# Token and unit transposes and slot products moved inside the gate/up and down groups of neighbouring experts

## The chip, the cores and the metric

The kernel runs on one NeuronCore of one Trainium2 chip. The metric is the device time of one launch in microseconds (us), lower is better; a profiled execution of the same program gives the trace.

## What is computed

One layer of a decoder trunk on 512 tokens of width 1024: a token mixer (an mLSTM branch and a latent attention branch, gated), cross-attention into 256 memory tokens, and a mixture of experts, each followed by a residual and a LayerNorm. All of it is in f32. The change lies in the mixture of experts, which is, in short:

```python
logits = xt @ w_router + b_router
top_val, top_idx = lax.top_k(logits, 4)
gate = softmax(top_val)
def expert(x, e):
    gu = x @ w_gu[e] + b_gu[e]
    glu, lin = gu[..., ::2], gu[..., 1::2]
    glu = minimum(glu, 7.0)
    lin = clip(lin, -7.0, 7.0)
    u = glu * sigmoid(1.702 * glu) * (lin + 1.0)
    return u @ w_dn[e] + b_dn[e]
```

Each of the 512 tokens goes to 4 of 32 experts; the experts' rows are weighted by the gate and added to the token. How many tokens an expert gets is known only at run time; on average it is 64.

## The kernel before

The first third of the span computes the mixer, the cross-attention and the router; the change leaves it alone. Then `experts` goes through the experts e = 0 to 31 in one unrolled loop, with down products one expert late (f = e - 1). The loop stands in a manual schedule: on PE, VectorE (DVE), ScalarE (ACT) and GpSimd (POOL) instructions run in the order in which the code issues them. Weights come in slabs of 128 x 1024 f32 (512 KB), 16 of gate/up and 8 of down for each expert, through a ring of 36 buffers (named raw, whi, wlo) that SP fills in the order of use; a buffer is free again when its last product has run.

The steps of one pass of the loop, with the lines of the code before:

- `up` (L1090): gate/up products of expert e, tokens stationary, weights streaming, in four quarters of two k each. An expert's tokens are cut into parts of 64, 32, 32 and 64; all but the first are inside branches on the token count (over 64: L1105, over 96: L1107, over 128: L1109). The result lies in four PSUM buffers of the tag gu, and for the last part in two of the tag y (tiles gux).
- `tokens` (L1059): PE transposes the gathered rows xg of expert e + 1 (tile xt), ACT copies them to xe. Second and third part are in branches (L1068, L1070).
- `routing` and `route_expert`: sixteen small products with one-hot matrices give the places and gates of expert e + 2 (tile sl; "slots" below), DVE reads them; POOL makes the next one-hots. `conds` then loads the next token count into registers of each engine (L1228).
- `gather` by POOL into xg for expert e + 2.
- `units` (L1121): DVE and ACT turn gate/up results into units (tiles mg, ml, mlx), the parts beyond 64 tokens first, each in its branch (L1126, L1127, L1128).
- `down` (L1168): down products of expert f into y, y2 (tag y) and y3, yx (tag gu), in two halves of four k each, with the same cuts by token count (L1172, L1174, L1176).
- `hidden` (L1135): PE transposes the units of expert e (tile ht), ACT copies them to hs, the stationary operand of the next down.
- `rows_out` (L1179): ACT and DVE add up the rows of expert f (tile ysb), POOL scatters them into the output sum.

PSUM has two buffers each of the tags y and tp (transposes and slots take tp) and four of gu, so that down's y is the bank that gate/up's overflow part had just before. A branch that is not taken lets the engine's sequencer wait for the work before it and signal in its place; the trace names such a releaser with a q (DVEq L1126, PEq L1107).

Of the kernel before, what the change touches and what calls it, by code (L numbers as in the profile page):

```python
# [109 lines left out]
class Trunk:  # L110
# [976 lines left out]
                for h in range(2):  # L1087
                    self.bias(e, n, h, j, out(h, j))

    def up(self, rv, e, x, w):  # L1090

        tc = self.tc
        b = [self.ps("gu", "gu") for _ in range(4)]
        bm = [self.ps("gux", "y") for _ in range(2)]

        def two(b):
            return lambda h, j: b[j][64 * h:64 * h + 64]

        def four(b):
            return lambda h, j: b[64 * j + 32 * h:64 * j + 32 * h + 32]  # L1100

        for q in range(4):
            ks = (2 * q, 2 * q + 1)
            self.up_part(e, ks, 64, x[:, :, 0:64], w, two(b))
            with tc.If(rv > 64):  # L1105
                self.up_part(e, ks, 32, x[:, :, 64:96], w, four(b[2]))
                with tc.If(rv > 96):  # L1107
                    self.up_part(e, ks, 32, x[:, :, 96:128], w, four(b[3]))
                    with tc.If(rv > 128):  # L1109
                        self.up_part(e, ks, 64, x[:, :, 128:192], w, two(bm))  # L1110
        return b, bm

    def some_units(self, g, l, pg, pl, by=1.0):
# [4 lines left out]
        nc.vector.tensor_scalar(l, pl, 8.0, -6.0, op0=OP.min, op1=OP.max)  # L1118
        nc.vector.scalar_tensor_tensor(l, l, by, g, op0=OP.mult, op1=OP.mult)

    def units(self, rv, b, bm, twice):  # L1121

        tc = self.tc
        g = self.mx.tile([128, 512], F32, name="mg", tag="mg", bufs=1)
        l, l2, lx = [self.mx.tile([128, 512], F32, name=n, tag=n, bufs=1) for n in ("ml", "ml2", "mlx")]
        with tc.If(rv > 64):  # L1126
            with tc.If(rv > 96):  # L1127
                with tc.If(rv > 128):  # L1128
                    self.some_units(g, lx, *bm)
                self.some_units(g[64:128], l2[64:128], b[3][0:64], b[3][64:128])  # L1130
            self.some_units(g[0:64], l2[0:64], b[2][0:64], b[2][64:128])
        self.some_units(g, l, b[0], b[1], twice)
        return l, l2, lx

    def hidden(self, rv, l, l2, lx):  # L1135
# [26 lines left out]
                r = 64 * (k % 2) + 32 * n  # L1162
                self.nc.tensor.matmul(o[r:r + 32], h[:, k], w(k)[:, ts(n, 512)], start=k < 2, stop=k > 5)  # L1163

    def down(self, rv, h, w):
        tc = self.tc
        y, y2 = [self.ps("y", "y") for _ in range(2)]
        y3, yx = [self.ps("yx", "gu") for _ in range(2)]  # L1168
        for q in range(2):
            ks = range(4 * q, 4 * q + 4)  # L1170
            self.down_64(ks, y, h[:, :, 0:64], w)
            with tc.If(rv > 64):  # L1172
                self.down_32(ks, y2, h[:, :, 64:96], w)
                with tc.If(rv > 96):  # L1174
                    self.down_32(ks, y3, h[:, :, 96:128], w)
                    with tc.If(rv > 128):  # L1176
                        self.down_64(ks, yx, h[:, :, 128:192], w)
        return y, y2, y3, yx

    def rows_out(self, rv, few, p, route):  # L1180
# [46 lines left out]
    def cond(self, c, *engines):  # L1227
        return self.nc.values_load(c[0:1, 0:1], engines=engines, min_val=0, max_val=512,  # L1228
                                   skip_runtime_bounds_check_because="a count of the 512 tokens")

    def experts(self):
        nc, tc, a = self.nc, self.tc, self.a
        p, cond = self.mx, self.cond
        PE, DVE, ACT, POOL = (mybir.EngineType.PE, mybir.EngineType.DVE, mybir.EngineType.Activation, mybir.EngineType.Pool)
        self.more_x = p.tile([64, 1024], F32, name="mrxg", bufs=1)
        nc.gpsimd.memset(self.more_x, 0.0)
        self.ys = [p.tile([128, 1024], F32, name=f"ysb{i}", bufs=1) for i in range(2)]
        for y in self.ys:
            nc.gpsimd.memset(y, 0.0)

        order = []
        for e in range(33):
            order += [(e, h, k) for k in range(8) for h in range(2) if e < 32]
            order += [(e - 1, 2, k) for k in range(8) if e]
        slabs, self.nfetch = {}, 0

        def fetch(n):

            for e, part, k in order[self.nfetch:self.nfetch + n]:
                slabs[e, part, k] = self.slab(a["wdn"][e, k] if part == 2 else a["wgu"][e, part, k])  # L1250
            self.nfetch += n

        def number(e):

            c = self.mx.tile([1, 1], I32, name="number", tag="number", bufs=4)
            nc.gpsimd.tensor_copy(c, self.count[0:1, e:e + 1])
            return c

        def conds(c):
            return cond(c, PE, ACT), cond(c, DVE, ACT), cond(c, POOL), cond(c, PE)  # L1260

        def more_gather(e):
            with tc.If(rv[e][2] > 128):
                self.gather(self.more_x, route[e][1][0])

        def routing(e):
            route[e] = self.route_expert(e, self.mx, self.oh)
            if e < 31:
                count[e + 1] = number(e + 1)
                self.oh = self.one_hots(e + 1, self.mx)  # L1270

        count = {0: number(0), 1: number(1)}
        route, rv, h = {0: self.first}, {0: conds(count[0])}, {}
        self.bias_rows()
        fetch(len(self.ring["s"][0]))
        more_gather(0)
        x = self.tokens(rv[0][0])
        self.oh = self.one_hots(1, self.mx)
        with tc.manual_schedule(engines={PE, DVE, ACT, POOL}):
            routing(1)  # L1280
            rv[1] = conds(count[1])
            self.gather(self.xg, route[1][0][0])
            more_gather(1)
            for e in range(33):
                f = e - 1
                if e < 32:
                    b, bm = self.up(rv[e][3], e, x, lambda h, k: slabs[e, h, k])
                    fetch(16)
                if e < 31:
                    x = self.tokens(rv[e + 1][0])  # L1290
                if e < 30:
                    routing(e + 2)
                    rv[e + 2] = conds(count[e + 2])
                    self.gather(self.xg, route[e + 2][0][0])
                    more_gather(e + 2)
                if e < 32:
                    l = self.units(rv[e][1], b, bm, route[e][2])
                if 0 < e:
                    out = self.down(rv[f][3], h[f], lambda k: slabs[f, 2, k])
                    fetch(8)  # L1300
                if e < 32:
                    h[e] = self.hidden(rv[e][0], *l)
                if 0 < e:
                    self.rows_out(rv[f][1], rv[f][2], out, route[f])
        self.overflow()

    def overflow(self):
# [174 lines left out]
```

## Time and profile before

| | us |
|---|---|
| median of 3 runs (lowest to highest) | 1924.85 (1924.28 to 1926.68) |
| profiled execution, its own time | 1923.97 |
| span of its trace | 1922.3 |
| PE busy | 1717.8 |
| DVE busy | 623.8 |
| ACT busy | 462.7 |
| POOL busy | 299.5 |

The mean granted TensorE clock over the span is 0.953 of full speed; HBM is read and written at 271 GB/s on average. The expert loop takes the stretch from about 629 to 1886. PE's idle time is listed in the trace with what ended it; PE busy is no measure of PE at its peak, since matmuls overlap and their time depends on the granted clock.

### The profile page before, as it was taken

To read this page: it belongs to the slowest core of one execution; us is meant where nothing else is said; L and a number is where in the kernel's file an instruction comes from. 1 tells how busy PE (TensorE), PEld (TensorE's weight loads), DVE (VectorE), ACT (ScalarE), POOL (GpSimd) and SP (SyncE) were. 2 spreads that over 40 slices of the span, in tenths; PEclk is the share of its full clock that TensorE was granted. 3 is DMA by queue.
4 is the path that set the end of the run, shared out by engine and by line. 5 is a ranking of instruction groups with operands and counts; after the bars stand their busy time and mean duration, and the time that the engine had idled before them with its cause. 6 is when DMAs were issued, how large, how long until landed. Compare 5 with 4: busy or idle time off the path is not lost. (4 is left out here: it accounts for less than half of the span.)

```text
span 1922.3 us, 26305 instructions
## 1 busy us (share of the span) xinstructions
PE 1717.8 (89%) x9564; PEld 854.1 (44%) x9564; DVE 623.8 (32%) x1319; ACT 462.7 (24%) x882; POOL 299.5 (16%) x413
## 2 busy tenths in 40 slices
PE   8998999999996788989999888888988898998892
PEld 6666888778975222332332232223322333233230
DVE  7855776467564212111121111111111102122113
ACT  5567555345431201110111111001001101111001
POOL 1000003420012212111101121112111112011202
PEclk9999999999997899999999999999999999999996
DMA  4213334655234999998657999899998998678973
GB/s 165 93 61 115 97 108 159 197 189 187 83 119 156 383 404 389 383 378 327 231 191 273 364 361 354 322 364 368 396 355 330 387 353 309 207 264 303 397 268 116
DMA packets 149257, 504.88 MB, mean 263 GB/s; under 512 B 21648, under 2 KB 24240, under 8 KB 149040
## 3 DMA queue, kind: packets, MB, share of 16 engines
q1 hardware_dynamic: 131632, 459.86, 63.9%
q0 software_dynamic: 17408, 42.02, 7.7%
q8 instruction: 150, 2.46, 0.5%
q14 instruction: 67, 0.55, 0.1%
HBM read 486.84 MB, written 33.29 MB: 271 GB/s over the span
## 5 line engine op out<-in xcount | busy, mean ns | idle before, releaser
L1084 PE MATMUL gu<-raw,xe 128*64 128x512 f32 (+1 forms) x2624 | 516.0, 600 | 24.2 <-PEq L1107 10.6
L1084 PEld LDWEIGHTS gu<-raw,xe 128*64 128x64 f32 (+1 forms) x2624 | 153.4, 127 | 337.3 <-issue 308.6
L1156 PE MATMUL y<-raw,hs 128*64 128x512 f32 x920 | 254.5, 701 | 31.4 <-DVEq L1127 8.2
L998 DVE TENSOR_REDUCE gs<-sl 128x1 f32<-128x3 f32 x32 | 5.1, 161 | 665.5 <-PE sl L996 665.4
L984 POOL TENSOR_SCALAR oh<-places,pm 128x192 bf16<-128x192 bf16 x128 | 97.2, 789 | 548.7 <-PE sl L996 527.4
L1065 ACT COPY xe<-xt 128x512 f32<-128x512 f32 x50 | 27.8, 588 | 596.6 <-PE xt L1056 596.6
L1156 PEld LDWEIGHTS y<-raw,hs 128*64 128x64 f32 x920 | 76.5, 160 | 191.9 <-issue 142.6
L1017 POOL DMA_INDIRECT based<-ysb,ixm x32 | 51.5, 1611 | 477.4 <-ACT ysb L1205 417.4
L128 DVE TENSOR_TENSOR wlo<-raw,whi 128x1024 fp32r<-128x1024 f32 (+2 forms) x81 | 86.9, 1075 | 45.2 <-ACT whi L128 44.9
L1141 ACT COPY hs<-ht 128x512 f32<-128x512 f32 (+1 forms) x55 | 26.5, 510 | 309.3 <-PE ht L1056 309.3
L128 ACT CAST whi<-raw 128x1024 fp32r<-128x1024 f32 (+2 forms) x81 | 75.4, 932 | 80.6 <-issue 19.0
L1084 PE MATMUL gu<-wlo,xe 128*64 128x512 f32 (+1 forms) x368 | 87.8, 594 | 3.3 <-PEq L1107 2.3
L1084 PE MATMUL gu<-whi,xe 128*64 128x512 f32 (+1 forms) x336 | 80.6, 602 | 5.6 <-PEq L1147 1.8
L1117 ACT ACTIVATE mg<-mg 128x512 f32<-128x512 f32 (+1 forms) x55 | 34.6, 630 | 127.2 <-DVE mg L1116 119.7
L1192 DVE TENSOR_TENSOR ysb<-ysb,y 32x512 f32<-32x512 f32 x30 | 20.4, 680 | 137.8 <-ACT ysb L1191 137.6
L1163 PE MATMUL y<-raw,hs 128*32 128x512 f32 x440 | 57.6, 598 | 0.0
L160 PE MATMUL g<-xTh,wlo 128*128 128x512 f32 x128 | 52.4, 410 | 2.8 <-DVE wlo L128 2.8
L158 PE MATMUL g<-xTh,whi 128*128 128x512 f32 x128 | 52.5, 410 | 0.0
L159 PE MATMUL g<-xTl,whi 128*128 128x512 f32 x128 | 52.0, 406 | 0.0
L1116 DVE TENSOR_SCALAR mg<-gu 128x512 f32<-128x512 f32 (+1 forms) x52 | 35.8, 689 | 47.0 <-ACTq L1126 18.3
L1084 PEld LDWEIGHTS gu<-wlo,xe 128*64 128x64 f32 (+1 forms) x368 | 25.2, 125 | 57.0 <-issue 53.2
L1204 DVE COPY ysb<-y 64x512 f32<-64x512 f32 x32 | 21.8, 683 | 80.5 <-PE y L1156 75.6
(494 smaller groups left out, 2793.3 us busy)
## 6 DMA issues: line engine op xcount, KB each, us to landing
raw<-in_wgu SPq DMA_DIRECT2D x406, 512.0 KB, 8.4
raw<-in_wdn SPq DMA_DIRECT2D x230, 512.0 KB, 10.1
wlo<-in_wgu SPq DMA_DIRECT2D x53, 512.0 KB, 10.0
whi<-in_wgu SPq DMA_DIRECT2D x53, 512.0 KB, 10.1
raw<-in_wt SPq DMA_DIRECT2D x27, 512.0 KB, 3.8
whi<-in_wdn SPq DMA_DIRECT2D x13, 512.0 KB, 10.5
wlo<-in_wdn SPq DMA_DIRECT2D x13, 512.0 KB, 10.0
tgd<-tg POOLq DMA_DIRECT2D x16, 256.0 KB, 2.8
```

The costliest lines, as they stand in the source:

```text
L128: return nc.scalar.copy(hi, src).ins, (lo_eng or nc.vector).tensor_sub(lo, src, hi.bitcast(F32)).ins
L158: mm(out, w[0], x[0], start=start, stop=False)
L159: mm(out, w[0], x[1], start=False, stop=False)
L160: mm(out, w[1], x[0], start=False, stop=stop)
L984: self.nc.gpsimd.tensor_scalar(oh[:, b], self.places, self.pm[:, b, e:e + 1], None, op0=OP.is_equal)
L1017: self.nc.gpsimd.indirect_dma_start(out=self.based, out_offset=bass.IndirectOffsetOnAxis(ap=ix[:, 0:1], axis=0), in_=y, in_offset=None, bo ...
L1065: nc.scalar.copy(x[:, :, c:c + n], self.turned(src, 8, "xt", first).rearrange("p (k t) -> p k t", t=n))
L1084: mm(out(h, j), x[:, k], w(h, k)[:, ts(j, 512)], start=k == 0, stop=False)
L1116: nc.vector.tensor_scalar(g, pg, 7.0, None, op0=OP.min)
L1117: nc.scalar.activation(g, g, AF.Gelu_apprx_sigmoid)
L1156: self.nc.tensor.matmul(o[64 * n:64 * n + 64], h[:, k], w(k)[:, ts(n, 512)], start=k == 0, stop=k == 7)
L1163: self.nc.tensor.matmul(o[r:r + 32], h[:, k], w(k)[:, ts(n, 512)], start=k < 2, stop=k > 5)
```

## The change

`up` takes a table of work to do behind its quarters, `units` and `down` take one function to call in their middle. Pass e of the loop then runs: first quarter of gate/up of e; unit transposes of f (`turn_units`); second and third quarter; slots of e + 2 (`next_slots`); fourth quarter; first half of down of f; units of e on DVE and ACT, and among them the token transposes of e + 1 and the gather of e + 2 (`next_tokens`); second half of down of f; rows of f. `units` now converts the part beyond 128 tokens first, in a branch of its own, then the first 64, and the parts between after the function has been called. The last unit transposes stand alone in the pass e = 32.

```diff
-    def up(self, rv, e, x, w):
+    def up(self, rv, e, x, w, between):
...
+            for work in between.get(q, ()):
+                work()
         return b, bm
...
-    def units(self, rv, b, bm, twice):
+    def units(self, rv, b, bm, twice, between):
...
+        with tc.If(rv > 128):
+            self.some_units(g, lx, *bm)
+        self.some_units(g, l, b[0], b[1], twice)
+        between()
         with tc.If(rv > 64):
+            self.some_units(g[0:64], l2[0:64], b[2][0:64], b[2][64:128])
             with tc.If(rv > 96):
-                with tc.If(rv > 128):
-                    self.some_units(g, lx, *bm)
                 self.some_units(g[64:128], l2[64:128], b[3][0:64], b[3][64:128])
-            self.some_units(g[0:64], l2[0:64], b[2][0:64], b[2][64:128])
-        self.some_units(g, l, b[0], b[1], twice)
...
-    def down(self, rv, h, w):
+    def down(self, rv, h, w, middle):
...
+            if q == 0:
+                middle()
...
+                def turn_units():
+                    if 0 < e < 33:
+                        h[f] = self.hidden(rv[f][0], *ls.pop(f))
+
+                def next_slots():
+                    if e < 30:
+                        routing(e + 2)
+                        rv[e + 2] = conds(count[e + 2])
+
+                def next_tokens():
+                    if e < 31:
+                        xs[e + 1] = self.tokens(rv[e + 1][0])
+                    if e < 30:
+                        self.gather(self.xg, route[e + 2][0][0])
+                        more_gather(e + 2)
+
+                def own_units(between):
+                    if e < 32:
+                        ls[e] = self.units(rv[e][1], *own, route[e][2], between)
+                    else:
+                        between()
+
                 if e < 32:
-                    b, bm = self.up(rv[e][3], e, x, lambda h, k: slabs[e, h, k])
+                    own = self.up(rv[e][3], e, xs.pop(e), lambda h, k: slabs[e, h, k], {0: [turn_units], 2: [next_slots]})
                     fetch(16)
-                if e < 31:
-                    x = self.tokens(rv[e + 1][0])
-                if e < 30:
-                    routing(e + 2)
-                    rv[e + 2] = conds(count[e + 2])
-                    self.gather(self.xg, route[e + 2][0][0])
-                    more_gather(e + 2)
-                if e < 32:
-                    l = self.units(rv[e][1], b, bm, route[e][2])
-                if 0 < e:
-                    out = self.down(rv[f][3], h[f], lambda k: slabs[f, 2, k])
+                else:
+                    turn_units()
+                if 0 < e < 33:
+                    out = self.down(rv[f][3], h[f], lambda k: slabs[f, 2, k], lambda: own_units(next_tokens))
                     fetch(8)
-                if e < 32:
-                    h[e] = self.hidden(rv[e][0], *l)
-                if 0 < e:
                     self.rows_out(rv[f][1], rv[f][2], out, route[f])
+                elif e == 0:
+                    own_units(next_tokens)
```

The order of PE at the end of gate/up, before the change (xt are the token transposes, sl the slots; a branch row stands where an `If` begins, an unconditional one where it ends):

```order
L1109 UNCONDITIONAL_BRANCH x2
L1107 UNCONDITIONAL_BRANCH
L1105 UNCONDITIONAL_BRANCH
L1056 MATMUL xt<-ident,xg 128x64 x8
L1068 COMPARE_AND_BRANCH
L1056 MATMUL xt<-ident,xg 128x64 x8
L1070 COMPARE_AND_BRANCH
L1056 MATMUL xt<-ident,mrxg 128x64 x8
L1070 UNCONDITIONAL_BRANCH x2
L1068 UNCONDITIONAL_BRANCH
L993 LDWEIGHTS oh
L993 MATMUL sl<-VT,oh 128x8
```

And in the changed program, on the same engine at the same place:

```order
L1109 UNCONDITIONAL_BRANCH x2
L1107 UNCONDITIONAL_BRANCH
L1105 UNCONDITIONAL_BRANCH
L1128 UNCONDITIONAL_BRANCH
L1159 MATMUL y<-wlo,hs 64x512 x2
L1159 MATMUL y<-raw,hs 64x512 x6
L1175 COMPARE_AND_BRANCH
```

Down's first products (y) now follow the last branch of gate/up; the xt rows stand behind the first half of down. The slots have moved ahead of the last quarter, where PE now reads (gu and bgu rows belong to gate/up; the register loads are those of the next token count):

```order
L996 LDWEIGHTS oh
L996 MATMUL sl<-VT,oh 64x8
L1233 TENSOR_LOAD number x2
L1084 MATMUL gu<-whi,xe 64x512 x4
L1084 MATMUL gu<-wlo,xe 64x512 x4
```

The two loads, which stood between the slots and down, now stand between the slots and the fourth quarter. On DVE, the units read before the change:

```order
L1126 COMPARE_AND_BRANCH
L1127 COMPARE_AND_BRANCH
L1128 COMPARE_AND_BRANCH
L1116 TENSOR_SCALAR mg<-gux 128x512
L1118 TENSOR_SCALAR mlx<-gux 128x512
L1119 SCALAR_TENSOR_TENSOR mlx<-mlx,mg 128x512
L1128 UNCONDITIONAL_BRANCH x2
L1116 TENSOR_SCALAR mg<-gu 64x512
```

And in the changed program:

```order
L1007 TENSOR_REDUCE gx<-sl 64x1
L1105 UNCONDITIONAL_BRANCH
L1233 TENSOR_LOAD number
L1128 COMPARE_AND_BRANCH
L1118 TENSOR_SCALAR mg<-gux 128x512
L1120 TENSOR_SCALAR mlx<-gux 128x512
L1121 SCALAR_TENSOR_TENSOR mlx<-mlx,mg 128x512
L1128 UNCONDITIONAL_BRANCH x2
L1118 TENSOR_SCALAR mg<-gu 128x512
```

The branch for more than 128 tokens is now the first and stands alone; the full 128-row conversion of the first 64 tokens follows it, where the 64-row ones came before.

## Rows read from the trace of the kernel before

**Rows 1.** The page, section 1: busy us (share of the span) and instructions of PE.

```profile
PE 1717.8 (89%) x9564; PEld 854.1 (44%) x9564; DVE 623.8 (32%) x1319; ACT 462.7 (24%) x882; POOL 299.5 (16%) x413
```

**Rows 2.** Waits of PE: waiting tile and line, releaser: us in total, times, longest.

```profile
PE y L1156 <- DVEq L1126: 15.6, 14, 1.4
...
PE sl L993 <- ACTq L1068: 10.8, 15, 0.7
PE sl L993 <- ACTq L1070: 10.7, 12, 0.9
PE y L1156 <- DVEq L1127: 8.2, 8, 1.1
...
PE y L1156 <- DVE mg L1116: 5.2, 3, 1.7
...
PE ht L1056 <- DVE ml L1119: 3.6, 1, 3.6
...
PE sl L993 <- ACT xe L1065: 2.0, 3, 0.7
```

**Rows 3.** Timeline of PE at one boundary: start, us, instructions, idle time before them.

```profile
786.68 0.99 PE L1056 MATMUL xt<-ident,xg 64*128 64x64 f32 x16 [0.30 <-PEq L1105]
788.57 0.46 PE L993 MATMUL sl<-VT,oh 128*128 128x8 bf16 x8 [0.90 <-ACTq L1070]
788.88 0.29 PE L996 MATMUL sl<-VT,oh 128*64 128x8 bf16 x8
790.19 5.35 PE L1156 MATMUL y<-raw,hs 128*64 128x512 f32 x16 [1.01 <-DVEq L1126]
795.70 2.80 PE L1156 MATMUL y<-raw,hs 128*64 128x512 f32 x12 [0.16 <-PEq L1172]
...
800.28 1.94 PE L1084 MATMUL gu<-whi,xe 128*64 128x512 f32 x8
```

**Rows 4.** Timeline of PE at another boundary.

```profile
1185.95 3.65 PE L1156 MATMUL y<-raw,hs 128*64 128x512 f32 x16 [1.09 <-DVEq L1127]
...
1195.02 1.51 PE L1084 MATMUL gu<-whi,xe 128*64 128x512 f32 x6 [0.43 <-PEq L1147]
```

**Rows 5.** Table of windows: us, busy by engine, then PEclk, DMA share, GB/s.

```profile
790.20:793.60 3.40, 3.40 (x12) 1.18 (x14) 2.16 (x3) 0.63 (x1) 3.23 (x4) 0.67 1.02 384
929.70:932.00 2.30, 1.48 (x13) 1.07 (x13) 0.67 (x1) 1.23 (x3) 0.00 (x0) 1.00 1.01 376
1186.00:1189.60 3.60, 3.60 (x16) 1.01 (x16) 3.29 (x5) 1.14 (x2) 3.14 (x4) 1.00 0.92 355
```

**Rows 6.** The page, section 5: down products from raw; count, busy us, mean ns, idle.

```profile
L1156 PE MATMUL y<-raw,hs 128*64 128x512 f32 x920 | 254.5, 701 | 31.4 <-DVEq L1127 8.2
```

**Rows 7.** Instructions of line L1228: register loads on PE's sequencer, ns min/median/max.

```profile
L1228 PEldq TENSOR_LOAD <-number x64: 297/303/488, 620.3 to 1811.2; - x64
```

**Rows 8.** The page, section 5: copies of xe, activation and conversion of the units.

```profile
L1065 ACT COPY xe<-xt 128x512 f32<-128x512 f32 x50 | 27.8, 588 | 596.6 <-PE xt L1056 596.6
...
L1117 ACT ACTIVATE mg<-mg 128x512 f32<-128x512 f32 (+1 forms) x55 | 34.6, 630 | 127.2 <-DVE mg L1116 119.7
...
L1116 DVE TENSOR_SCALAR mg<-gu 128x512 f32<-128x512 f32 (+1 forms) x52 | 35.8, 689 | 47.0 <-ACTq L1126 18.3
```

**Rows 9.** SP's slab issues until 800.28: count, KB each, median us to landing.

```profile
raw<-in_wgu SPq DMA_DIRECT2D x78, 512.0 KB, 11.8
raw<-in_wdn SPq DMA_DIRECT2D x37, 512.0 KB, 11.2
...
wlo<-in_wgu SPq DMA_DIRECT2D x11, 512.0 KB, 10.1
whi<-in_wgu SPq DMA_DIRECT2D x10, 512.0 KB, 10.2
```

**Rows 10.** Timeline of PE around an expert with all branches taken.

```profile
975.80 1.02 PE L1056 MATMUL xt<-ident,xg 64*128 64x64 f32 x16
...
980.06 6.55 PE L1156 MATMUL y<-raw,hs 128*64 128x512 f32 x16 [1.74 <-DVE mg L1116]
```

More of the change, by code (lines that the diff above doesn't have):

```diff
@@ L1276, in experts @@
         more_gather(0)
-        x = self.tokens(rv[0][0])
+        xs, ls = {0: self.tokens(rv[0][0])}, {}
         self.oh = self.one_hots(1, self.mx)
```

## The prediction

> **What bounds the kernel now.** The page first: TensorE (PE) is busy 89% of the span [rows 1], so time can come only from PE's own idle stretches, or from products that run faster. The list of PE's waits says where the idle stretches are. In the expert stage the same places return once per expert: the slot products (sl) stand until ScalarE (ACT) has copied the transposed tokens, and the first down product (y) stands until VectorE (DVE) has passed, or worked through, the branches of the units [rows 2]. The timeline of one expert boundary shows them in order: token transposes, a wait of 0.90 us, slots, a wait of 1.01 us, and only then the down group, whose first sixteen products take 5.35 us; the second half, 0.16 us on, is quick again [rows 3]. At another boundary, the same sixteen products take 3.65 us [rows 4]. The table of windows tells why: the granted clock is 0.67 (a mean of the levels 2.4 and 1.2 GHz) over the slow half and 1.00 over the quick one [rows 5]. So PE drops to the lower level behind the stretch of transposes, slots and waits, and the down group pays. Behind the shorter break at the units' transposes, 929.70 to 932.00, the clock is 1.00 [rows 5].
>
> What does not bound: DMA. Before product groups PE hardly ever waits for a slab, though the 16 DMA engines are full in places, as from 790.20 to 793.60 with a share of 1.02 and 384 GB/s [rows 5]; a rival below takes this up.
>
> **What the change is worth, part by part.** No product, transpose, slot or copy is added or removed; they are moved.
>
> *Slots into gate/up, behind the third quarter.* The buffer that sl takes was then last read by ACT for the units' transposes, two quarters earlier (at least 7.3 us: two times 3.65). So the waits of sl on ACT go: 10.8 + 10.7 + 2.0 = **23.5 us** [rows 2]. The first routing ahead of the loop is unchanged. What the slots lose is cover: the two register loads of the next count behind them, 0.303 us each on PE's sequencer [rows 7], ran under the wait for DVE; now the last quarter stands behind them. They are issued while the second half of the slots runs, 0.29 us [rows 3], so 2 x 0.303 - 0.29 = 0.32 us shows, with the restart some 0.35 (an estimate); 30 times, **-10.5 us**. Bounds: 0 if the sequencer is ahead, 30 x 0.9 = 27 if a wait as long as the present one stays.
>
> *Down directly behind gate/up.* DVE has passed the branch for more than 128 tokens before the last quarter ends, since the slots' reductions now come a quarter earlier and this branch stands first. The waits of y go: 15.6 + 8.2 + 5.2 = 29.0 [rows 2]. Three experts hold more than 128 tokens; there y must wait until DVE has read the overflow's bank, 0.689 us for one conversion [rows 8], and the signals around it, about 1.0; so 29.0 - 3.0 = **26.0 us**.
>
> *The clock.* The largest group of down products, 920 of the 1024 that write y with 64 columns, is busy 254.5 us [rows 6]. Sixteen undisturbed take 3.65 us [rows 4], so 920 would take 209.9; the excess is 44.6, and I take 44 for all. It is won if none of the new breaks lets the clock fall. They are: units' and token transposes, mostly some 1 us as at 786.68, and slots, 0.6 us, each with a branch gap of 0.16 to 0.43 on either side [rows 3, 4]. Nearly all are shorter than the 2.3 us of the break of [rows 5] that left the clock at 1.00, and dense products stand on both sides. **44 us**; bounds 0 (below, a rival) and 44.6 x 1024 / 920 = 50.
>
> *Token transposes between the halves of down.* They take the branch gap that the halves have today, 0.16 at 795.70 [rows 3], and the gap now in front of them falls to down: no net change. Behind them a branch gap becomes visible that the wait of sl had covered. Its nearest row is the gap behind the units' transposes, 0.43 where a second part was taken [rows 4]; where none is, the 0.16 of [rows 3]. The waits of sl tell how many there are of each: 12 behind the branch of the second part, 15 behind the first, 3 with a third part [rows 2]. 12 x 0.43 + 18 x 0.16 = **-8 us**; bounds 30 x 0.16 = 5 and 30 x 0.43 = 13. The copies of xe on ACT have the second half of down (3.65 us or more) as cover; two of 0.588 us are 1.2 [rows 8]. ACT has the units' activation queued ahead of them, which ends a conversion of 0.689 and its own 0.630 after gate/up [rows 8], and so before the first half does.
>
> *Units' transposes into gate/up, behind the first quarter.* Same number, same branches: zero. Their sources were made during the second half of down, and the copy to hs has three quarters as cover; if that cover were gone, a wait of about 0.6 us for each part. The first expert's transposes wait 3.6 us for the units today [rows 2]; that goes, and the next tokens' copies now stand behind the units' activation there, 0.630 + 2 x 0.588 = 1.8: **+1.8 us**.
>
> *Gather, scatter, SP.* The gather into xg is issued in the middle of down and needed one expert later (the loop's 1257 us over 32 experts make 39); the fetches of slabs keep their order. Zero, with the DMA rival as the reserve.
>
> *Tile shapes.* At 975.80 the token transposes follow gate/up with no idle time at all, where every branch was taken [rows 10]; a change from 64-column products to transposes then cost nothing that the row shows, and I put it at zero. The Trainium skill, "TensorEngine Tiling (Array Packing)", section "Key Properties", speaks against the change: changing the tiling mode, not just the tile, drains TensorE. By that rule the two more changes that each expert now has would not be free; the price stands among the rivals. I go by the row, and most of these places stand at a branch anyway.
>
> Sum: 23.5 + 26.0 + 44 + 1.8 - 10.5 - 8 = 76.8 us. The profiled execution took 1923.97 (span 1922.3), 0.9 below the median of the three runs shown. 1923.97 - 76.8 = **1847 us**, some 4%. A measurement of this kernel can tell about 0.2% from no change.
>
> **Rivals.**
> *The clock falls all the same.* If the breaks inside the groups are enough, the 44 are not won and the waits alone count: 1923.97 - 32.8 = 1891. For it: three experts have token transposes in three parts, and the clock fell behind the stretch of 3.5 us from 786.68 to 790.19 [rows 3, 5]. Against it: the clock of 1.00 around the break at 929.70. A fall at half of the experts would give 1869.
>
> *Every change of tile shape costs.* Each expert changes between 64-column products and transposes or slots six times instead of four. If each costs a restart as short as the 0.16 us at 795.70 [rows 3], 31 x 2 x 0.16 = 10 us are lost: 1857. This is what the rule of the page above would come to. Against it stands the row at 975.80 [rows 10], one place of one kind.
>
> *Weights become the bound.* At 800.28, when the sixth expert's gate/up begins [rows 3], SP had issued 78 + 11 + 10 = 99 gate/up slabs and 37 or more of down [rows 9]; 80 and 32 had been used. So the lead is 24 slabs. One lands 11.8 us after its issue, and takes 1.4 us at 384 GB/s, so 9 are on the way and 15 have landed, worth 21 us. The change takes 2.5 us from each of the five experts before, 12: it should hold. If it does not, here and in the other stretches at full DMA (a dozen experts in all), about 12 x 2.4 = 29 us are lost: 1876.
>
> *Slower: down waits for the units.* The y bank is the one that the overflow of gate/up had, and y waits for DVE. If DVE's signal came only after a whole conversion (three steps of DVE at 0.689, ACT's 0.630 among them [rows 8], about 3.0 us with signals), there would be 31 x 3.0 = 93 where 29 stood, right behind the group, and the clock would go on falling: 1923.97 - 23.5 + 64 + 18.5 = 1983. It decides against the change from a mean wait of (29.0 + 23.5 - 18.5) / 31 = 1.1 us per expert if the clock still falls, 2.5 us if not. For it: the row at 980.06, 1.74 us, where the branch was taken [rows 10]. Against: only three experts are like it.
>
> *The moves do nothing*, because the compiler orders PE otherwise: the order shows them done.
>
> **How the numbers follow.** Forecast 0.62 (its own range 1834 to 1862 by the bounds of the gaps), clock falls all the same 0.12, tile shapes 0.10, weights 0.09, slower 0.05, nothing 0.02. The range reaches up over the cases of tile shapes, of the weights and of a clock half won, 1832 to 1878; it leaves out the full loss of the clock, the slower case and nothing, 0.19. Faster 0.93, same 0.02, slower 0.05.
>
> **What would show it.** The waits of sl on ACT and of y on DVE gone from PE's list, but for three of about 1 us; sixteen down products in 3.65 us everywhere and a granted clock of 0.99 over the stage; a gap near 0.35 us behind the slots; no wait of gate/up for landing slabs above a few us. I am wrong if the clock's rows still dip once per expert, if y heads the list of waits, or if gate/up waits for DMA.

## The result, and the profile after

The changed kernel takes 1848.78 us in the median of 4 runs (1848.27 to 1851.46), against 1924.93 before: a ratio of 0.9606, with an interval of 0.9589 to 0.9622. Predicted were 1847.0. The profiled execution took 1848.27 with a span of 1846.5, so profile against profile the change is worth 1923.97 - 1848.27 = 75.7 us.

The page of the changed kernel, its row of PE and the row of the largest group of down products, answers to [rows 1] and [rows 6]:

```profile
PE 1673.2 (91%) x9564; PEld 855.8 (46%) x9564; DVE 622.8 (34%) x1319; ACT 462.2 (25%) x882; POOL 299.6 (16%) x413
...
L1159 PE MATMUL y<-raw,hs 128*64 128x512 f32 x920 | 211.3, 597 | 17.4 <-PEq L1107 4.3
```

The 920 products are busy 211.3 us where they took 254.5. PE is busy 44.6 us less in all, for the same 9564 instructions. Why is in the table of windows for one long stretch of the expert stage, where the third number from the end is the granted clock. Before the change (PE alone):

```profile
684.00:1811.00 1127.00, 1014.74 (x5990) 0.96 0.89 332
```

And in the changed kernel:

```profile
684.00:1811.00 1127.00, 1034.15 (x6304) 364.88 (x6304) 186.85 (x389) 134.01 (x237) 172.73 (x201) 1.00 0.93 351
```

The clock no longer dips: its records show 25 falls to 0.50 in the expert stage before, and none after. The stretch holds 314 more of PE's instructions. PE's waits answer to [rows 2]. These are the ones that speak of the predicted terms, and those that are put down to a slab, but for two more of 0.3 us each:

```profile
PE gu L1084 <- issue: 6.3, 26, 0.4
PE sl L993 <- PEq L1107: 6.0, 10, 0.7
...
PE y L1159 <- PEq L1070: 4.2, 9, 0.7
...
PE gu L1084 <- DMA raw<-in_wgu: 2.3, 7, 0.5
PE gu L1084 <- DVE ysb L1197: 2.1, 1, 2.1
PE y L1159 <- PE gux L1076: 2.0, 3, 0.7
...
PE y L1159 <- DMA raw<-in_wdn: 1.7, 4, 0.6
PE gu L1084 <- DMA raw<-in_wdn: 1.4, 3, 0.6
PE y L1159 <- DMA raw<-in_wgu: 1.3, 3, 0.5
```

No slot waits for ACT, and no row names DVE for a down product. The three large experts do still wait for it, though the list puts their 2.0 us down to gux: at one of them y starts at 956.12, 0.10 us after DVE's first conversion of the overflow has ended (955.33 and 0.69 us long). What mostly stands ahead of sl and y otherwise is PE's own sequencer leaving a branch (PEq). The first row shown is new, gate/up's last quarter waiting for "issue": the register loads behind the slots. One expert boundary of the timeline, which answers to [rows 3]:

```profile
810.60 0.46 PE L993 MATMUL sl<-VT,oh 128*128 128x8 bf16 x8 [0.56 <-PEq L1109]
810.92 0.29 PE L996 MATMUL sl<-VT,oh 128*64 128x8 bf16 x8
811.62 3.65 PE L1084 MATMUL gu<-raw,xe 128*64 128x512 f32 x16 [0.41 <-issue]
...
820.25 3.65 PE L1159 MATMUL y<-raw,hs 128*64 128x512 f32 x16 [0.54 <-DMA raw<-in_wgu]
824.05 0.68 PE L1056 MATMUL xt<-ident,xg 64*128 64x64 f32 x8
824.88 3.65 PE L1159 MATMUL y<-raw,hs 128*64 128x512 f32 x16
```

Both halves of down take 3.65 us now.

Where the 75.7 us come from can be added up on the timeline, from the start of one kind of work on PE to the start of the next kind, from the first gate/up product to the last down product. So each kind holds the idle time behind it:

| us, start to start | before | after | difference | predicted |
|---|---|---|---|---|
| token transposes | 53.2 | 37.1 | -16.1 | -13.7 |
| slots | 55.5 | 26.0 | -29.5 | -22.1 |
| gate/up | 717.8 | 725.5 | +7.7 | +3.0 |
| units' transposes | 40.9 | 41.2 | +0.3 | 0 |
| down | 388.2 | 347.1 | -41.1 | -44 |
| ahead of the stage | | | +2.9 | 0 |
| sum | | | -75.8 | -76.8 |

The predicted column sorts the prediction's terms by the place where they show: tokens -23.5 + 8 + 1.8, slots -29.0 - 3.6 + 10.5, gate/up 3.0 for the three large experts. Ahead of the stage, where the change moves nothing, the first gate/up product starts at 632.34 instead of 629.44; that start differs by up to 3.7 us between this kernel and those below, too.

### The profile page after: what moved, and what is told of

Same layout as the page of the kernel before. It is cut to its first block, busy times and chain, and to the rows that moved or that the text cites. A ratio compares the mean times of both kernels' runs of the same rounds, so it can differ in the third digit from the quotient of the medians.

```text
span 1846.5 us, 26477 instructions
## 1 busy us (share of the span) xinstructions
PE 1673.2 (91%) x9564; PEld 855.8 (46%) x9564; DVE 622.8 (34%) x1319; ACT 462.2 (25%) x882; POOL 299.6 (16%) x413
## 5 line engine op out<-in xcount | busy, mean ns | idle before, releaser
L1084 PE MATMUL gu<-raw,xe 128*64 128x512 f32 (+1 forms) x2624 | 514.2, 598 | 27.5 <-issue 4.6
L1084 PEld LDWEIGHTS gu<-raw,xe 128*64 128x64 f32 (+1 forms) x2624 | 157.8, 126 | 316.4 <-issue 289.2
L1159 PE MATMUL y<-raw,hs 128*64 128x512 f32 x920 | 211.3, 597 | 17.4 <-PEq L1107 4.3
L1159 PEld LDWEIGHTS y<-raw,hs 128*64 128x64 f32 x920 | 71.7, 136 | 126.4 <-issue 89.2
L1011 POOL DMA_INDIRECT xg<-x2d,ixm x32 | 36.0, 1124 | 305.9 <-PEq L1068 178.1
```

The source lines that it names most:

```text
L1011: return self.nc.gpsimd.indirect_dma_start(out=xg, out_offset=None, in_=self.x2d, in_offset=bass.IndirectOffsetOnAxis(ap=ix[:, 0:1], axis= ...
L1084: mm(out(h, j), x[:, k], w(h, k)[:, ts(j, 512)], start=k == 0, stop=False)
L1159: self.nc.tensor.matmul(o[64 * n:64 * n + 64], h[:, k], w(k)[:, ts(n, 512)], start=k == 0, stop=k == 7)
```

## The experiments

Theory A is the prediction's: the waits go, the clock stays up because the stretch without 64-column products is cut into short breaks, and the exits cost a little. Rival B is that the direct contact of down with gate/up is what counts, so that anything between the two lets the clock fall. Further theories are named where they come up.

**One part alone, or one undone.** Four kernels. The first is the kernel before with only the slots and their register loads moved behind the third quarter:

```diff
-                    b, bm = self.up(rv[e][3], e, x, lambda h, k: slabs[e, h, k])
+                    b, bm = self.up(rv[e][3], e, x, lambda h, k: slabs[e, h, k], {2: [next_slots]})
```

> The kernel before with one move alone: the slots and the register loads go behind the third quarter of gate/up; token transposes stay between gate/up and down, units' transposes behind down, units in their old order. Theory A (length): PE lost its time to two waits and to a clock that fell behind one long stretch without dense products; with the slots gone from it, that stretch is token transposes and two branch gaps, 1 to 1.7 us, the waits of sl (23.5 us) and nearly all of y (29) go, and the clock stays up: 1850 to 1858 us, y from raw busy some 211 us. Rival B (contact): down has to follow gate/up directly, or the clock falls: the waits go but 44 us of clock do not, 1893 to 1902 us, y from raw busy some 255 us.

It took 1853.25 us, a ratio of 0.9634 (0.9606 to 0.9662). The slots alone bring 70.5 of the change's 76 us; the granted clock over the stage is 1.00 here as well, although the token transposes still stand between gate/up and down. So direct contact is not needed. The other three undo one part each. The slots back between gate/up and down:

```diff
-{0: [turn_units], 2: [next_slots]})
-                    fetch(16)
+{0: [turn_units]})
+                    fetch(16)
+                    next_slots()
```

> The changed kernel with the slots put back between gate/up and down; token and units' transposes stay inside the groups. Theory A: the slots' reductions by DVE stand again in front of the branch that y waits for, about 1.0 us per expert instead of the 0.2 us behind the slots now, 30 x 0.8 = 24 us; the stretch without dense products is some 2.2 us, about as long as the one that left the clock up, so the clock stays at 1.00 or falls in a few places: 1868 to 1885 us. Rival B: the clock falls at most experts, 24 + 44 = 68 us, 1910 to 1920 us.

1874.42 us, as A said, 25.6 more than the change. The wait is back: the list of this kernel's waits of PE, over the stretch of the windows above, begins with

```profile
PE y L1159 <- DVEq L1128: 26.2, 25, 1.4
```

The fall of the clock is not back at most experts, as its table of windows shows:

```profile
684.00:1811.00 1127.00, 1018.80 (x6236) 356.88 (x6234) 187.17 (x387) 132.45 (x234) 174.67 (x201) 1.00 0.93 350
```

The 1.00 is rounded: the stretch holds two falls of 3.4 us, one behind sixteen units' transposes with 1.20 us of idle time (from 989.3), one behind slots between waits of 0.77 and 1.38 us (from 1163.4). So an idle wait of about 1 us behind the slots, 25 times in the row above, hardly ever lowered the clock by itself. In the kernel before it had the token transposes and their own wait in front of it. And the gains overlap: without the slots' move the two others bring 1923.76 - 1874.42 = 49.3 us, without them it brings 70.5, since either saves the clock.

The token transposes back between gate/up and down:

```diff
+                    next_tokens()
...
-                    out = self.down(rv[f][3], h[f], lambda k: slabs[f, 2, k], lambda: own_units(next_tokens))
+                    out = self.down(rv[f][3], h[f], lambda k: slabs[f, 2, k], lambda: own_units(lambda: None))
```

> The changed kernel with the token transposes put back between gate/up and down; slots and units' transposes stay inside the groups. Theory A: the same transposes and branch gaps at another place, no wait, clock at 1.00: within 6 us of the changed kernel, 1843 to 1855 us. Rival B: the clock falls behind them, 44 us: 1885 to 1895 us.

And the units' transposes back behind down:

```diff
-{0: [turn_units], 2: [next_slots]})
+{2: [next_slots]})
...
+                    turn_units()
                     self.rows_out(rv[f][1], rv[f][2], out, route[f])
```

> The changed kernel with the units' transposes put back behind down, as before the change; slots and token transposes stay inside the groups. Theory A: the units of 65 and more tokens are converted behind the tokens' copies and may be late at the end of down by up to 1 us for a dozen experts: 1849 to 1862 us, clock at 1.00. Rival B: down still follows gate/up directly, so nothing is lost either, 1849 us; the two theories do not differ here, the run tells what this move is worth.

1850.77 us (1848.71 to 1852.84) and 1852.81 (1852.10 to 1853.52). Both lie where A put them; the first can't be told from the change itself. With the slots moved, each of these two moves brings little.

**Is it the length of the stretch, or the idle time in it?** Twenty transposes of the identity ahead of the token transposes make that break longer than 3 us without a wait:

```diff
+        for _ in range(extra):
+            self.nc.tensor.transpose(pt[:, 0:128], self.ident, self.ident)
```

> The changed kernel with 20 additional transposes of the identity (128x128, thrown away) in front of each expert's token transposes, between the halves of down. At some 0.11 us each (the interval of the units' transposes) they cost 2.2 us per expert by themselves, 31 x 2.2 = 68 us, and make one stretch of about 3.8 us without dense products, as long as the one before the change. Theory A (length): the clock falls behind it at most experts, 1.7 us each, another 30 to 50 us: 1945 to 1970 us, and y from raw busy 235 us or more. Rival D (waits): the clock fell because PE stood idle, and transposes keep it up: 1849 + 68 = 1917 us, clock 1.00.

1918.70 us (1917.53 to 1922.13, 8 runs): the theory of the length, mine, fell, and D, idle time, stood so far. The timeline of PE at one boundary:

```profile
833.46 3.65 PE L1161 MATMUL y<-raw,hs 128*64 128x512 f32 x16 [0.54 <-PEq L1111]
837.26 2.38 PE L1056 MATMUL xt<-ident 128*128 128x128 f32 x20 [0.15 <-PEq L1177]
839.57 0.71 PE L1058 MATMUL xt<-ident,xg 64*128 64x64 f32 x8
840.43 3.65 PE L1161 MATMUL y<-raw,hs 128*64 128x512 f32 x16
```

And the windows over the transposes and over the products behind them:

```profile
837.26:839.57 2.31, 2.31 (x21) 2.14 (x21) 0.00 (x0) 0.00 (x0) 0.00 (x0) 1.00 1.01 397
840.50:844.00 3.50, 3.50 (x16) 1.16 (x16) 2.06 (x3) 1.66 (x3) 1.10 (x1) 1.00 1.03 411
```

Three microseconds of nothing but transposes, and the clock is 1.00 in them and behind them. At two experts with many tokens the break lasts 4.48 us, longer than 26 of the 30 breaks with token transposes and slots before the change; the windows over one of these and over the products behind it:

```profile
920.30:924.70 4.40, 3.91 (x44) 3.62 (x44) 0.00 (x0) 1.07 (x2) 0.68 (x1) 1.00 1.01 339
924.80:928.30 3.50, 3.50 (x17) 1.01 (x16) 2.12 (x4) 1.74 (x3) 0.34 (x1) 1.00 1.01 412
```

In the whole stage the clock falls once, in gate/up behind a wait of 2.13 us for an output sum (1651.07), and behind no stretch of transposes. The extra transposes cost their own time and no more. The same twenty spread over three breaks, 7, 7 and 6 of them:

> The changed kernel with the same 20 additional transposes per expert, 7 in front of the token transposes, 7 in front of the units' transposes, 6 in front of the slots. Each break becomes about 0.7 us longer, some 2.4 us at most for usual experts. Theory A: the direct cost alone, 68 us, and the clock stays at 1.00 but for a few places: 1912 to 1925 us. If the number of transposes mattered and not the length of a stretch, it would come out like the lumped one.

1911.28 us, a little under the range, and again the clock falls only once, behind the same wait of 2.13 us (1640.13). Spread out they cost 62 us instead of 70: the six ahead of the slots make the slots' work 37.9 us from start to start, 11.9 more than the 26.0 without them, 0.40 each time where the 0.12 us of one make 0.7. That would fit register loads that now run under them.

**Idle time, or products with few columns?** The stretch that lowered the clock held both. First the kernel before with eight transposes in the place of the wait for DVE:

```diff
+                    fill = self.ps("fl", "tp")
+                    for _ in range(8):
+                        nc.tensor.transpose(fill[:, 0:128], self.ident, self.ident)
                     rv[e + 2] = conds(count[e + 2])
```

> The kernel before, with eight transposes of the identity into a buffer of their own between the slots and down, thirty times: at 0.12 us each (2.38 us for 20 in the run with 20 extra transposes) they fill about 1.0 us, nearly the 1.01 us for which y stands there waiting for DVE. Nothing else moves, and the stretch between gate/up and down stays as long. Theory D (PE standing idle is what lets the clock fall): the granted clock stays at 1.00 over the stage, the y<-raw row falls from 254 to about 211 us busy, and the time comes to 1924 - 44 plus up to 6 for the restart behind the filler, 1880 to 1890. Rival A (the length of the stretch without products of 64 columns lets it fall, or where it stands): the row stays near 250, 1924 to 1932. If the clock is saved at half of the places, about 1905.

1908.92 us (0.9919, 0.9890 to 0.9947): the middle case. PE's timeline at one boundary:

```profile
754.24 0.68 PE L1056 MATMUL xt<-ident,xg 64*128 64x64 f32 x8 [0.30 <-PEq L1105]
755.64 0.46 PE L993 MATMUL sl<-VT,oh 128*128 128x8 bf16 x8 [0.72 <-ACTq L1068]
755.96 0.29 PE L996 MATMUL sl<-VT,oh 128*64 128x8 bf16 x8
756.18 1.09 PE L1295 MATMUL fl<-ident 128*128 128x128 f32 x8
757.21 1.85 PE L1156 MATMUL y<-wlo,hs 128*64 128x512 f32 x4
```

The windows right behind the filler, here and at another boundary; here the clock is still halved, there it holds:

```profile
757.40:760.80 3.40, 3.40 (x10) 0.98 (x9) 1.73 (x3) 0.63 (x1) 3.24 (x4) 0.50 1.05 381
1182.80:1186.40 3.60, 3.60 (x16) 1.03 (x16) 3.27 (x5) 1.11 (x2) 3.16 (x4) 1.00 0.83 325
```

The row of the down products on the page stands between the 254.5 and the 211.3 us of the two kernels:

```profile
L1156 PE MATMUL y<-raw,hs 128*64 128x512 f32 x920 | 224.3, 629 | 10.7 <-PEq L1174 4.2
```

The clock falls 17 times in the stage where it fell 25 times. Work in the place of idle time, in a kernel that keeps the old order and, but for 0.15 us at each expert, the old length, wins back 19.6 us in the down groups by the sum from start to start (368.6 instead of 388.2), nearly half of the 41.1. What is left in the stretch is the other wait, for ACT, and the slots. So then the slots by themselves: the changed kernel with the first eight of their sixteen products issued nine times. These are 64 more for each expert; the expectation counts 128.

```diff
-        for n, c in ((128, 0), (CAP - 128, 128)):
+        for n, c in ((128, 0), (CAP - 128, 128)) * (1 if pool is self.route else 9):
```

> The changed kernel with the slot products issued nine times instead of once inside gate/up (the same sums, started anew): 128 more products of 8 columns for each of 30 experts, which keep PE issuing, with nearly no columns streamed. By the 0.46 us of the first 8 and the 0.29 us for the second 8 they take some 2.3 to 4 us each time, a stretch like the one that dropped the clock in the kernel before, but without an idle wait. Theory D1 (only idle time lowers the clock; a tiny product counts as work): granted clock 1.00, so 1849 + 30 x (2.3 to 4) = 1918 to 1969, and gate/up's last quarter keeps its 597 ns per product. Theory D2 (products of 8 columns count like idle time): the clock falls behind most of these stretches and the last quarter of gate/up pays some 1.5 us each time: the gu<-raw row grows from 514 us busy by 30 or more, and the time is 40 or so longer, 1960 to 2010.

2000.34 us (1.0393, 1.0346 to 1.0440), by theory D2. PE's timeline:

```profile
835.02 3.71 PE L993 MATMUL sl<-VT,oh 128*128 128x8 bf16 x72 [0.56 <-PEq L1109]
838.59 0.29 PE L996 MATMUL sl<-VT,oh 128*64 128x8 bf16 x8
839.04 5.35 PE L1084 MATMUL gu<-raw,xe 128*64 128x512 f32 x16 [0.16 <-issue]
```

The windows over the slots and over products behind them:

```profile
835.02:838.80 3.78, 3.78 (x80) 3.44 (x80) 0.00 (x0) 0.00 (x0) 0.00 (x0) 1.00 0.84 289
839.95:843.36 3.41, 3.41 (x11) 1.21 (x9) 0.00 (x0) 0.00 (x0) 2.11 (x3) 0.50 0.47 187
```

And the page's row of gate/up's products:

```profile
L1084 PE MATMUL gu<-raw,xe 128*64 128x512 f32 (+1 forms) x2624 | 548.4, 627 | 24.3 <-PEq L1107 4.2
```

PE is busy without a gap for 3.78 us, and the clock is halved right behind: the next sixteen products take 5.35 us, the figure of [rows 3]. The gate/up row is 34.2 us longer than the 514.2 of the changed kernel. From start to start the slots take 96.4 us more than in the changed kernel and gate/up 53.0 more. The clock falls at 29 of the 30 experts, at one of them (1748.11) with no idle time on either side of the slots, while behind breaks of transposes of the same length it held. So the slots alone can bring the fall about. Whether it is their eight columns or their bf16 operands was not tested.

**The loads behind the slots.** The next count's register loads moved behind the first 64-column products of the last quarter:

```diff
             self.up_part(e, ks, 64, x[:, :, 0:64], w, two(b))
+            for work in between.get((q, "in"), ()):
+                work()
...
-{0: [turn_units], 2: [next_slots]})
+{0: [turn_units], 2: [next_slots], (3, "in"): [next_conds]})
```

> The changed kernel with the register loads of the next count moved from directly behind the slots to behind the first part of the last quarter's products, where PE's sequencer runs ahead of PE. If the gap behind the slots (6.3 us in all in the list of waits, 26 times) is that of the loads, it goes: 1842 to 1846 us. If it is the change from slots to products, nothing moves: 1849 us.

1835.19 us (0.9536, 0.9517 to 0.9555), 13.6 less than the change and so better than expected. The timeline at the boundary that was shown above for the changed kernel:

```profile
805.20 0.46 PE L993 MATMUL sl<-VT,oh 128*128 128x8 bf16 x8 [0.56 <-PEq L1111]
805.52 0.29 PE L996 MATMUL sl<-VT,oh 128*64 128x8 bf16 x8
805.64 3.65 PE L1084 MATMUL gu<-raw,xe 128*64 128x512 f32 x16
```

Gate/up starts 0.12 us after the second row of slots instead of 0.70. From start to start the slots take 13.7 us in all, not 26.0: the loads cost 12.3 us, 0.41 for each of thirty, twice the 6.3 of the list. The list counts idle time from the modelled end of the last slot product, 0.29 us after its group's start, but the next product can start before that end; the overlap that is lost shows in no wait. Over the whole stage this kernel gains 10.3 us from start to start (1166.6 against 1176.9); 3.7 of the profiled gain lie ahead of the stage.

**Fewer breaks.** Gate/up in two halves of four k instead of four quarters, the slots and loads behind the first part of the second half:

```diff
-        for q in range(4):
-            ks = (2 * q, 2 * q + 1)
+        for q in range(2):
+            ks = range(4 * q, 4 * q + 4)
...
-{0: [turn_units], 2: [next_slots]})
+{0: [turn_units], (1, "in"): [next_conds, next_slots]})
```

> The changed kernel with gate/up in two halves of four k instead of four quarters of two, the loads and the slots behind the first part of the second half, the units' transposes behind the first half. Two chains of branches per expert go, each of which leaves a gap of 0.16 to 0.56 us where a branch is not taken; 31 x 2 x 0.35 = 22 us, and 6 us for the loads: 1818 to 1830 us, clock at 1.00. Against it: slabs are given back in groups of eight instead of four, so the lead of the weights shrinks by a few us from a smallest value that the lists of waits put at more than nothing; if gate/up or down then waits for DMA, up to 20 us come back.

1811.72 us (1811.44 to 1814.59, 4 runs; 0.9411, 0.9396 to 0.9427), the fastest of all, 37 us under the change and below the range that was expected. Its timeline where the slots stand:

```profile
804.83 0.63 PE L1076 MATMUL gu<-bgu,esel 128*64 128x512 bf16 x4
805.39 0.47 PE L993 MATMUL sl<-VT,oh 128*128 128x8 bf16 x8
805.72 0.29 PE L996 MATMUL sl<-VT,oh 128*64 128x8 bf16 x8
805.95 3.64 PE L1084 MATMUL gu<-raw,xe 128*32 128x512 f32 x32
```

And the first row of its list of PE's waits, over the stretch of the windows above:

```profile
PE y L1161 <- DVEq L1130: 8.4, 11, 0.8
```

The slots have no gap on either side, and gate/up has half as many branches to leave: its work takes 683.5 us from start to start instead of 725.5, and the idle time behind its products falls from 48.6 to 22.4 us. The row of waits shows what it pays: experts with few tokens have nothing between slots and down, so y waits for DVE again, 8.4 us in that row and 2.15 more at one place (1265.20), where the clock falls too. These waits lie in the slots' 30.2 us from start to start.

## Why the prediction was right

**The waits of the slots, -23.5, with -8 for the exit behind the tokens.** Right: the tokens' work got 16.1 us shorter from start to start where -13.7 was due.

**The waits of down, -26.0.** The mechanism was right, the size too small. The slots' work got 29.5 us shorter where 22.1 were due, although the loads cost 12.3 and not 10.5. Three things were missed in reading [rows 2]. The list of before has these rows, too:

```profile
PE y L1156 <- DMA raw<-in_wgu: 2.0, 2, 1.1
...
PE y L1156 <- DVEq L1128: 1.2, 1, 1.2
...
PE y L1156 <- DMA whi<-in_wgu: 1.1, 1, 1.1
```

One more expert waits for DVE, and 3.1 us of y's waits are put down to slabs of gate/up, which y doesn't read; both belong to the same place. And the list starts at a product's modelled end, which hides what overlap would have given, as the loads showed. The three large experts wait for their bank 2.0 us instead of the 3.0 allowed.

**The clock, 44.** Right in size: 254.5 - 211.3 = 43.2 us in that row. Down's difference in the table is smaller, since the idle time behind its products, mostly branch exits, grew from 16.3 to 20.0 us. The condition that the prediction put on it, "if none of the new breaks lets the clock fall", held, but its reason was half wrong. It took the length of a break without 64-column products as what counts. Breaks of 3.13 to 4.48 us made of transposes left the clock alone, 3.78 us of slots lowered it. In the stretch of [rows 3] that speaks for the two waits of 0.90 and 1.01 us and the slots between them, and against the 0.99 us of transposes as the cause; no run holds a stretch of that length made of these narrower transposes alone. The rival of a clock that falls all the same is out, with 1.00 over the stage.

**The exit behind the slots, -10.5.** 12.3 us, worked out from two durations and an estimate; the list's 6.3 would have been the worse guide.

**Units' transposes and gather, 0.** 41.2 against 40.9 us. What the prediction left out lies in gate/up, +7.7 where 3.0 were due. Summed over the timeline, the idle time behind gate/up's products grew from 39.1 to 48.6 us: branch exits with the shortest gaps from 35.4 to 38.5, waits put down to slabs from 1.1 to 3.8, the waits of the three large experts for their bank 0 to 2.0, others from 2.7 to 4.3. The products themselves gave back the difference of 1.8. So the branch exits inside gate/up and the waits for slabs, whose growth the prediction put at nothing, are what it missed there.

**The other rivals.** Weights: 7.3 us of waits in the list after are put down to a slab, 5.7 before; a part of them is branch exits, as the 0.54 us at 820.25: at the same place in the run with twenty transposes (833.46) the same 0.54 are put down to PE's own branch. 29 us were not lost. Tile shapes: in the run with twenty transposes PE goes over from shape 128*128 to 64*128 at 839.57 with no idle time in front, and without the loads gate/up follows the slots at once (805.64). So no trace here bears out the 10 us of that rival, nor a drain as the Trainium skill, "TensorEngine Tiling (Array Packing)", section "Key Properties", has it for a change of mode, as far as the place of a transpose or a slot product shows it. Down waiting for units: 2.0 us, three times.

The forecast of 1847 against 1848.78 was closer than its terms, and that is luck. Slots and tokens gained 9.8 more than predicted, and gate/up, down, the start of the stage and the units' transposes gave back 10.8 (4.7 + 2.9 + 2.9 + 0.3).

## What to carry to other kernels

Put small dependent steps (a routing product, a transpose) between dense products whose operands are already there, two groups ahead of their reader, so that the answer of the other engine is awaited under the next dense group; what is gained is the wait and, where the granted clock fell behind it, the time of the products that follow: here about as much again. Look for the second half in the busy time of a product row at the same count, not among the idle times. Then count the branches and register loads that the moved step brings along: each is a gap of some tenths of a microsecond, and the kernel with half as many branch chains in gate/up and with the loads moved was 37 us faster still.

## What had not been expected of the hardware

- Of two kinds of small work on TensorE, f32 transposes of 128 columns kept the granted clock at 1.00 (20 of them, 2.38 us, in breaks of up to 4.48 us), while behind 3.78 us of unbroken 8-column bf16 products it fell to 0.50, at 29 of 30 experts. How much of either it takes was not measured.
- Two register loads of 0.304 us on PE's sequencer behind the slots cost 0.41 us for each expert although the slots in front of them run for 0.46 us, and behind sixteen dense products they cost almost nothing: the slots' work lost 12.3 us of 26.0, gate/up's grew by 2.1.
